# RWKV scan: inverse triangles multiplied in ahead of the recurrence, first inversion on VectorE, gate product inside the scan

## The chip, the cores and the metric

One core of a Trainium2 chip runs the whole program. The metric is the device time of one execution in microseconds (us); for one core that is the time from its first to its last instruction and what the launch adds to it. All arithmetic of the part in question is in fp32 (4 bytes); a few large products split each operand into a high and a low fp32r part and take three matmuls.

## The reference, cut to what matters

A two-block transformer on 512 tokens of width 1024 (and 256 context tokens). The change lies in one mixer of the second block, a bidirectional RWKV layer of 16 heads of size 64. What it computes per direction z, head h and token t (S is a 64x64 state):

```python
def _wkv_step(S, inp):
    r_t, w_t, k_t, v_t, a_t, b_t = inp
    sa = jnp.einsum('zbhvk,zbhk->zbhv', S, a_t)
    S = S * w_t[..., None, :] + sa[..., :, None] * b_t[..., None, :] + v_t[..., :, None] * k_t[..., None, :]
    return S, jnp.einsum('zbhvk,zbhk->zbhv', S, r_t)

def rwkv_out(y, h, xx, r, k_mod, v, mu, ln_g, ln_b, r_k, g1, g2, wo):
    y = layernorm(y, ln_g.reshape(RWKV_HEADS, RWKV_HEAD), ln_b.reshape(RWKV_HEADS, RWKV_HEAD), GN_EPS)
    bonus = jnp.einsum('bthk,zbthk->bth', _heads(r) * r_k, _heads(k_mod))
    y = y.astype(r.dtype) + bonus[..., None] * _heads(v)
    xg = h + xx * mu[5]
    gate = jax.nn.sigmoid(xg @ g1) @ g2
    return (y.reshape(bsz, n, d) * gate) @ wo
```

Here g1 is 1024 x 160 and g2 160 x 1024. The scan first runs over the 256 context tokens and goes on over the 512 tokens.

## The kernel before, in words

`rwkv_project` (L1913) forms r, k, v, q and the gate and stores them to DRAM, feature rows first, in the tensors `rw_r`, `rw_k` and so on. Its last piece is the gate: ACT takes the sigmoid of the 160 x 512 product (L2057), both factors are split into high and low parts, and for each of 8 blocks of 128 features PE runs 6 matmuls (L2074 to L2077), ACT copies the result (L2079) and SP stores it to `rw_g` (L2080).

`_RwkvScan` (L2107) then works in 8 head pairs p (128 features each). Tokens are cut in chunks of 64; 4 chunks make a unit, and a pair has three units u (0 is the context, 1 and 2 the tokens), so 12 chunk steps a pair and 96 in all. Inside a chunk the recurrence is solved in closed form, which needs the inverse of a unit lower triangle (64x64) for each chunk, direction and head.

- `pre` (L2288) makes the decayed operands AR and BK and the strict triangles of a pair; `load_tri` (L2397) brings the 32x32 diagonal blocks through DRAM into a layout of 96 partitions; `subst` (L2410) inverts them there in 31 dependent rounds of two instructions on GpSimd (POOL, L2420 and L2424, 62 instructions); `back` (L2427) returns them through DRAM to XT, and `merge` (L2442) builds the 64x64 inverses with 32x32 matmuls.
- `prep` (L2485) makes the products AAk and AAr of a unit, BKn by transposes, the values UV, and `intra` (L2548) multiplies AAk into UV: this is the right side of the chunk's system.
- `scan` (L2581) is the recurrence, a chain over engines: two matmuls of the state S with AR into `ry` (L2600, or L2605 in unit 0), a VectorE (DVE) add of the right side into `rz` (L2609), four matmuls with the inverse XT (L2616), an ACT copy into UV (L2620), four matmuls into the state's sums `sps` (L2625), and DVE's update of S with the decay (L2636, L2634 in a pair's first step). Beside the chain stand ACT's decayed copy (L2643), four matmuls that add the chunk's own part to `ry` (L2649) and the copy to yn (L2653).
- `out` (L2656) turns and normalises a finished pair, loads the pair's rows of `rw_g` (L2664) and multiplies (L2697).

The order of the work: `run` (L2128) emits the chain's pieces one by one at a high priority (offset 400) and, between them, the work of `beside` (L2156), that is the inversion, `pre`, `prep`, `merge` and `out` of neighbouring pairs; a scheduler then fixes one order for each engine, and every engine takes its instructions in that order. Before step 0 of a pair its `merge` has to be done. PSUM pools: ry 2, u 1, s 1, aa 2, tp 2 banks.

## Time and profile before

| what | value |
|---|---|
| median of 3 runs | 4190.04 us (4182.6 to 4209.11) |
| profiled execution | 4201.93 us |
| its span, first to last instruction | 4200.0 us |
| projections of the RWKV layer end, gate stage | about 2855 to 2880 us of the span |
| ahead of the first scan step | 2880 to 2978 us |
| scan steps of the 8 pairs | 2978 to 3587 us |
| PE busy share of the span | 90% |

Times in rows count from the span's start. PE is TensorE's matmuls, DVE VectorE, ACT ScalarE, POOL GpSimd; SPq is the queue that issues the DMAs. A busy PE includes the latency of its matmuls, and an fp32 matmul of this program shows as two records, so 8 records are 4 matmuls. "Clock" below is TensorE's granted clock: 1.00 is 2.4 GHz, 0.50 is 1.2 GHz.

### The profile page before, as it was taken

To read this page: it belongs to the slowest core of one execution; us is meant where nothing else is said; L and a number is where in the kernel's file an instruction comes from. 1 tells how busy PE (TensorE), PEld (TensorE's weight loads), DVE (VectorE), ACT (ScalarE), POOL (GpSimd) and SP (SyncE) were. 2 spreads that over 40 slices of the span, in tenths; PEclk is the share of its full clock that TensorE was granted. 3 is DMA by queue.
4 is the path that set the end of the run, shared out by engine and by line. 5 is a ranking of instruction groups with operands and counts; after the bars stand their busy time and mean duration, and the time that the engine had idled before them with its cause. 6 is when DMAs were issued, how large, how long until landed. Compare 5 with 4: busy or idle time off the path is not lost. (4 is left out here: it accounts for less than half of the span.)

```text
span 4200.0 us, 56465 instructions
## 1 busy us (share of the span) xinstructions
PE 3774.0 (90%) x22550; PEld 2588.1 (62%) x22550; DVE 1838.8 (44%) x3646; ACT 1322.6 (31%) x2612; POOL 683.8 (16%) x889
## 2 busy tenths in 40 slices
PE   7979999999999979998789997996788899688986
PEld 6747778756777869887333334774667777433332
DVE  3445345565534545334422225445657655511112
ACT  3334224344323433233111113424456555200001
POOL 1002000200201010001100002002555342200001
PEclk9969999999999989999899998997768769799998
DMA  3213553212452322122799996342211212499997
GB/s 110 81 38 117 182 192 105 81 32 76 144 179 82 101 70 68 52 102 79 294 406 391 398 404 236 93 152 66 54 40 43 60 48 79 185 394 415 415 413 306
DMA packets 324825, 711.86 MB, mean 169 GB/s; under 512 B 79616, under 2 KB 251904, under 8 KB 299728
## 3 DMA queue, kind: packets, MB, share of 16 engines
q1 hardware_dynamic: 308704, 658.43, 43.1%
q0 software_dynamic: 15856, 49.79, 3.4%
q8 instruction: 179, 2.93, 0.3%
q14 instruction: 86, 0.70, 0.1%
HBM read 666.64 MB, written 47.55 MB: 170 GB/s over the span
## 5 line engine op out<-in xcount | busy, mean ns | idle before, releaser
L266 PE MATMUL mmps<-xH,wH 128*128 128x512 f32 (+1 forms) x1384 | 552.0, 401 | 11.2 <-ACT xH L359 9.4
L268 PE MATMUL mmps<-xH,wL 128*128 128x512 f32 (+1 forms) x1384 | 543.9, 394 | 2.4 <-DVE wL L245 2.4
L267 PE MATMUL mmps<-xL,wH 128*128 128x512 f32 (+1 forms) x1384 | 544.8, 394 | 0.0
L1488 PE MATMUL bgps<-wg,bxT 128*64 128x512 f32 (+2 forms) x1040 | 471.5, 597 | 0.9 <-issue 0.9
L1489 PE MATMUL bgps<-wu,bxT 128*64 128x512 f32 (+1 forms) x896 | 398.2, 597 | 21.1 <-DMA wu<-in_moe_w_up_dram 20.8
L244 ACT ACTIVATE wH<-wraw 128x512 fp32r<-128x512 f32 (+3 forms) x473 | 265.0, 620 | 481.4 <-PE mmps L267 270.6
L245 DVE TENSOR_TENSOR wL<-wraw,wH 128x512 fp32r<-128x512 f32 (+3 forms) x473 | 328.6, 739 | 193.6 <-ACT wH L244 193.0
L266 PEld LDWEIGHTS mmps<-xH,wH 128*128 128x128 f32 (+1 forms) x1384 | 259.9, 188 | 92.4 <-ACT wH L244 12.4
L268 PEld LDWEIGHTS mmps<-xH,wL 128*128 128x128 f32 (+1 forms) x1384 | 259.9, 188 | 66.1 <-DVE wL L245 3.9
L1505 PE MATMUL byps<-wd,bhT 128*64 128x512 f32 (+2 forms) x1040 | 297.0, 658 | 1.1 <-ACT bhT L1496 1.1
L267 PEld LDWEIGHTS mmps<-xL,wH 128*128 128x128 f32 (+1 forms) x1384 | 260.2, 188 | 59.9 <-issue 1.4
L1488 PEld LDWEIGHTS bgps<-wg,bxT 128*64 128x64 f32 (+2 forms) x1040 | 139.0, 137 | 206.7 <-issue 200.3
L1490 ACT ACTIVATE bh<-bgps 64x512 f32<-64x512 f32 (+2 forms) x65 | 38.3, 590 | 641.2 <-PE bgps L1489 543.0
L1489 PEld LDWEIGHTS bgps<-wu,bxT 128*64 128x64 f32 (+1 forms) x896 | 111.9, 128 | 132.7 <-issue 91.6
L1491 DVE TENSOR_TENSOR bh<-bgps,bh 64x512 f32<-64x512 f32 (+1 forms) x56 | 38.6, 690 | 335.7 <-ACT bh L1490 335.7
L1505 PEld LDWEIGHTS byps<-wd,bhT 128*64 128x64 f32 (+2 forms) x1040 | 87.9, 147 | 157.8 <-issue 152.1
L2420 POOL TENSOR_TENSOR isub<-xT,rwX 96x31 f32<-96x31 f32 (+15 forms) x248 | 140.6, 567 | 262.0 <-DMA xT<-rwd 243.2
L1454 POOL DMA_INDIRECT xg<-hnat,ix x65 | 62.8, 967 | 640.1 <-PE bxps L1476 602.9
L2424 POOL TENSOR_TENSOR rwX<-rwX,isub 96x31 f32<-96x31 f32 (+15 forms) x248 | 155.5, 627 | 19.4
L2807 POOL TENSOR_TENSOR sqs<-sqs,sq 128x512 f32<-128x512 f32 (+1 forms) x60 | 82.3, 1372 | 392.8 <-ACT sq L2800 386.4
L266 PE MATMUL mmps<-mH,pH 128*128 128x512 f32 (+2 forms) x336 | 124.1, 372 | 12.0 <-ACT pH L244 9.1
L532 POOL TENSOR_TENSOR ffng<-ffng,rstd 128x512 f32<-128x512 f32 x44 | 57.8, 1316 | 452.2 <-ACT ffng L531 439.9
(746 smaller groups left out, 7529.6 us busy)
## 6 DMA issues: line engine op xcount, KB each, us to landing
wg<-in_moe_w_gate_dram SPq DMA_DIRECT2D x64, 2048.0 KB, 23.1
wu<-in_moe_w_up_dram SPq DMA_DIRECT2D x61, 2048.0 KB, 20.1
wd<-in_moe_w_down_dram SPq DMA_DIRECT2D x61, 2048.0 KB, 19.2
adaw<-in_ada_w_dram SPq DMA_DIRECT2D x48, 1024.0 KB, 5.0
wraw<-in_ffn_w_gate_dram SPq DMA_DIRECT2D x22, 1024.0 KB, 5.4
wraw<-in_ffn_w_up_dram SPq DMA_DIRECT2D x22, 1024.0 KB, 5.5
wraw<-in_ffn_w_down_dram SPq DMA_DIRECT2D x20, 1024.0 KB, 5.0
wraw<-in_ga_w_in_dram SPq DMA_DIRECT2D x16, 1024.0 KB, 5.5
```

The costliest lines, as they stand in the source:

```text
L244: self.nc.scalar.activation(H, src, AF.Copy)
L245: self.nc.vector.tensor_tensor(L, src, H.bitcast(F32), OP.subtract)
L266: nc.tensor.matmul(out, lh, rh, start=first, stop=False)
L267: nc.tensor.matmul(out, lh, rl, start=False, stop=False)
L268: nc.tensor.matmul(out, ll, rh, start=False, stop=last)
L1454: self.gathered = self.nc.gpsimd.indirect_dma_start(out=x[:m, :], out_offset=None, in_=hnat, in_offset=bass.IndirectOffsetOnAxis(ap=it, ax ...
L1488: nc.tensor.matmul(og, xT[:, k, :m], wg[:, k, :], start=k == 0, stop=k == KD - 1, skip_group_check=True)
L1489: nc.tensor.matmul(ou, xT[:, k, :m], wu[:, k, :], start=k == 0, stop=k == KD - 1, skip_group_check=True)
L1505: nc.tensor.matmul(o[j], hT[:, k, :m], wd[:, k, j * 512 : (j + 1) * 512], start=k == 0, stop=k == 3, skip_group_check=True)
L2420: G.tensor_tensor(o, Lt[:96, :j, j : j + 1].to_broadcast((96, j, n)), X[:96, j : j + 1, j:].to_broadcast((96, j, n)), OP.mult,)
L2424: G.tensor_tensor(X[:96, :j, j:], X[:96, :j, j:], o, OP.add)
L2807: K.nc.gpsimd.tensor_tensor(self.acc, self.acc, t, OP.add)
```

## The change

The inverse is no longer a link of the recurrence. For each unit, `prep` turns the state's operand by matmuls with the identity, multiplies the inverse into that operand (which is then copied back into AR) and into the right side UV (a new function `solve`), so that a chunk step goes from `ry` straight to `sps`: the add writes UV itself. Units 1 and 2 are solved inside `prep`, unit 0 behind `merge`. The first pair's inversion runs on DVE and not on POOL. The gate's second factor is no longer applied ahead of the scan: only the sigmoid (160 rows) is stored, and `out` multiplies it with 128 columns of g2 in two fp32 matmuls (128 and 32 rows deep). PSUM's u bank goes to tp.

```diff
@@ rwkv_project
-                nc.sync.dma_start(raw[: b - a], io["rw_g2"][a:b, :].rearrange("p (k f) -> p k f", f=P))
-                gate.append((b - a, sg, raw, wH, wL))
+                nc.sync.dma_start(dr["g"][a:b, :], sg[: b - a, :T])
...
-        for f in range(KD):
-            ps = self.pp.tile([P, 512], F32, tag="mm", name="mmps")
-            for i, (n, H, L, wH, wL) in enumerate(parts):
-                self.mm3(ps, wH[:n, f], wL[:n, f], H[:n, :T], L[:n, :T], i == 0, i == 1)
-            st = hp.tile([P, TA], F32, tag="st", name="st", bufs=3)
-            nc.scalar.activation(st[:, :T], ps, AF.Copy)
-            nc.sync.dma_start(dr["g"][f * P : (f + 1) * P, :], st[:, :T])
@@ _RwkvScan: pools, beside, setup, subst
-    NSCAN = 36
+    NSCAN = 24
-        self.pp = _Tagged(K.pool("rwps", space=PSUM, ctx=c), {"ry": 2, "u": 1, "s": 1, "aa": 2, "tp": 2})
+        self.pp = _Tagged(K.pool("rwps", space=PSUM, ctx=c), {"ry": 2, "s": 1, "aa": 2, "tp": 3})
...
+        if n == 0:
+            for _ in inv:
+                pass
+            self.back(0)
+            self.marks.add(("subst", 0))
...
-            mg = self.merge(n)
+            mg = (w for g in (self.merge(n), self.cur[n]["solve"]) for w in g)
...
-                with self.K.tc.high_priority(offset=400) if n == 7 else ExitStack():
+                with self.K.tc.high_priority(offset=400) if n in (0, 7) else ExitStack():
...
+        nc.sync.dma_start(self.glow, self.dr["g"][P:, :])
...
-        G, X, Lt = self.nc.gpsimd, self.X, self.Lt
+        G, X, Lt = self.nc.gpsimd if p else self.nc.vector, self.X, self.Lt
@@ prep, at the end of intra(u)
+            A.activation(I, ps, AF.Copy)
...
+                    PE.matmul(
+                        ps[64 * (1 - pr) : 64 * (1 - pr) + 64, (2 * z + m) * P : (2 * z + m + 1) * P],
+                        AR[:, 4 * z + j, (1 - pr) if u else 0, :], K.ident, start=True, stop=True, skip_group_check=True,
+                    )
+            V.tensor_copy(An, ps)
+            yield 0.6
+            L["solve"] = solve(u, An, I, UV)
+            if u:
+                yield from L["solve"]
+
+        def solve(u, An, I, UV):
+            XT, AR = L["XT"], L["AR"][u]
...
+                        PE.matmul(
+                            wps[j % 2][64 * h : 64 * h + 64, (2 * z + m) * 64 : (2 * z + m) * 64 + 64],
+                            An[r0 : r0 + 64, (2 * z + m) * P + 64 * h : (2 * z + m) * P + 64 * h + 64],
+                            XT[r0 : r0 + 64, u * 8 + z * 4 + h * 2 + m, :], start=True, stop=True, skip_group_check=True,
+                        )
...
+                        PE.matmul(
+                            ps[r0 : r0 + 64, o : o + 64], XT[r0 : r0 + 64, u * 8 + z * 4 + h * 2 + m, :],
+                            I[r0 : r0 + 64, o : o + 64], start=True, stop=True, skip_group_check=True,
+                        )
+            for q, w in enumerate(wps):
+                V.tensor_copy(AR[:, q::2, (1 - q) if u else 0, :], w[:, :256].rearrange("p (x i) -> p x i", i=64))
             A.activation(UV[64:, :, 0::2, :], p4[64:], AF.Copy)
             A.activation(UV[:64, :, 1::2, :], p4[:64], AF.Copy)
@@ scan
-                    V.tensor_tensor(rz[Uh], ry[Uh, :256].rearrange("p (z f) -> p z f", z=2), rhs, OP.add)
...
-                        PE.matmul(
-                            up[Uh, z * P + 64 * h : z * P + 64 * h + 64], XT[:, u * 8 + z * 4 + h * 2 + m, :],
-                            rz[:, z, 64 * h : 64 * h + 64], start=True, stop=True, skip_group_check=True,
-                        )
-                A.activation(rhs, up[Uh, :256].rearrange("p (z f) -> p z f", z=2), AF.Copy)
+                    V.tensor_tensor(uv, ry[Uh, :256].rearrange("p (z f) -> p z f", z=2), uv, OP.add)
@@ out
-        nc.sync.dma_start(gt, self.dr["g"][p * P : (p + 1) * P, :])
+        nc.sync.dma_start(gt, self.dr["g"][:P, :])
+        for t, a, b in ((g2, 0, P), (g2low, P, 160)):
+            nc.sync.dma_start(t, self.io["rw_g2"][a:b, p * P : (p + 1) * P])
...
-        V.tensor_tensor(yT, gt, yT, OP.mult)
+        ps = self.ps()
+        PE.matmul(ps, g2, gt, start=True, stop=False)
+        PE.matmul(ps, g2low, self.glow, start=False, stop=True)
+        V.tensor_tensor(yT, ps, yT, OP.mult)
```

Three places show how the order moves. In the changed kernel the line numbers are lower by 12 from `load_pre` to `products`, higher by 23 in `scan` and by up to 29 in `out`.

SP at the start of the scan, before (rw_g is the gate, ink, inq, inr and rwlora are what the first `pre` reads):

```order
L1986 DMA rw_r<-st 128x512 x5
L2080 DMA rw_g<-st 128x512 x8
L2241 DMA rwmask<-in_cst_dram 128x256
L2241 DMA rwflip<-in_cst_dram 128x128
L2241 DMA rwblk_19376<-in_cst_dram 128x128
L2242 DMA rwreset<-in_cst_dram 128x256
L2279 DMA ink<-rw_k 128x768
L2279 DMA inq<-rw_q 128x768
L2279 DMA inr<-rw_r 128x512
L2281 DMA rwloraw<-in_rw_w_dram 128x128
```

and now (rwX is the corner of a tile that holds the low 32 rows of the gate's first factor):

```order
L1987 DMA rw_r<-st 128x512 x5
L2059 DMA rw_g<-rwsg 128x512
L2059 DMA rw_g<-rwsg 32x512
L2228 DMA rwmask<-in_cst_dram 128x256
L2228 DMA rwflip<-in_cst_dram 128x128
L2228 DMA rwblk_19278<-in_cst_dram 128x128
L2229 DMA rwreset<-in_cst_dram 128x256
L2246 DMA rwX<-rw_g 32x512
L2267 DMA ink<-rw_k 128x768
L2267 DMA inq<-rw_q 128x768
L2267 DMA inr<-rw_r 128x512
L2269 DMA rwloraw<-in_rw_w_dram 128x128
```

The eight stores of the gate are gone; in their place stand two, and a load that reads one of them back stands ahead of the pair's loads.

DVE at the first inversion now (L2408 and L2412 are the inversion's two instructions, the others belong to `pre` of the second pair and `prep` of the first; before, POOL had the inversion and DVE's queue only the others):

```order
L2322 SCALAR_TENSOR_TENSOR cs<-rwreset,sg 128x256 x2
L2408 TENSOR_TENSOR isub<-xT,rwX 96x31
L2323 TENSOR_TENSOR sg<-cs,sg 128x512
L2412 TENSOR_TENSOR rwX<-rwX,isub 96x31
L2563 COPY AAk<-rwtpps 128x512
L2408 TENSOR_TENSOR isub<-xT,rwX 96x60
L2336 TENSOR_TENSOR km<-km,ink 128x256
L2412 TENSOR_TENSOR rwX<-rwX,isub 96x30x2
L2336 TENSOR_TENSOR km<-km,ink 128x256
L2408 TENSOR_TENSOR isub<-xT,rwX 96x87
```

The inversion begins behind the work already queued and alternates with 33 other instructions up to its 34th; the rest of it stands alone.

DVE between the last state update of unit 0 (L2636, L2659 now) and the add of unit 1's first step (L2609, L2643 now), in a middle pair. Before:

```order
L2636 SCALAR_TENSOR_TENSOR S<-rwsps,P,SP 128x128 x2
L2335 TENSOR_TENSOR sg<-cs,sg 128x512
L2347 SCALAR_TENSOR_TENSOR bb<-th,inq 128x256
L2348 TENSOR_TENSOR km<-km,ink 128x256
L2349 SCALAR_TENSOR_TENSOR BK<-bb,E_23697 128x4x128
L2353 SCALAR_TENSOR_TENSOR ARc<-inq,sg 128x256 x2
L2359 TENSOR_TENSOR BK<-km,E_23697 128x4x2x64
L2609 TENSOR_TENSOR rwrz_19395<-rwryps,UV 64x256
```

and now (L2594 is the solved operand's copy, L2703 and L2705 the statistics of `out`):

```order
L2659 SCALAR_TENSOR_TENSOR S<-rwsps,P,SP 128x128 x2
L2347 TENSOR_TENSOR BK<-km,E_23946 128x4x2x64
L2594 COPY ARl<-rwtpps 128x4x64 x2
L2369 TENSOR_TENSOR xT<-rwaaps,rwmask 128x2x128 x2
...
L2322 SCALAR_TENSOR_TENSOR cs<-rwreset,sg 128x256 x2
L2336 TENSOR_TENSOR km<-km,ink 128x256
L2703 BN_STATS gbs<-AAk 128x6 x8
L2705 BN_AGGR gmv<-gbs 128x2 x8
L2323 TENSOR_TENSOR sg<-cs,sg 128x512
...
L2347 TENSOR_TENSOR BK<-km,E_24109 128x4x2x64
L2708 RECIPROCAL grs<-grs 128x8
L2643 TENSOR_TENSOR UV<-rwryps,UV 64x2x128
```

More than twice the work now stands between the two instructions of the chain.

## Rows read from the trace of the kernel before

**Rows 1.** Stretches: us, busy us (instructions) of PE, PEld, DVE, ACT, POOL, clock, DMA.
```profile
2855.00:2888.00 33.00, 21.33 (x49) 11.00 (x48) 2.95 (x8) 8.36 (x14) 1.69 (x4) 0.63 0.37 129
...
2921.00:2978.00 57.00, 32.47 (x443) 27.76 (x443) 41.46 (x66) 20.00 (x41) 41.01 (x68) 0.62 0.22 50
2978.00:3587.00 609.00, 559.31 (x6375) 440.75 (x6376) 372.26 (x951) 340.23 (x762) 264.48 (x443) 0.80 0.20 52
```

**Rows 2.** Timeline of the gate stage: start, duration, engine, line, instruction.
```profile
2856.01 1.06 ACT L2057 ACTIVATE rwsg<-thps 128x512 f32<-128x512 f32 x2
...
2879.34 0.60 ACT L2079 ACTIVATE st<-mmps 128x512 f32<-128x512 f32 x1 [2.56 <-PE mmps L268]
...
2888.38 1.22 PE L2309 MATMUL rwtpps<-rw_tw,rwloraw 64*128 64x256 f32 x4 [9.12 <-DMA rwloraw<-in_rw_w_dram]
```

**Rows 3.** Timeline of POOL, first and last instruction of the first inversion.
```profile
2921.25 0.25 POOL L2420 TENSOR_TENSOR isub<-xT,rwX 96x31 f32<-96x31 f32 x1 [40.60 <-DMA xT<-rwd]
...
2964.53 0.24 POOL L2424 TENSOR_TENSOR rwX<-rwX,isub 96x31 f32<-96x31 f32 x1
```

**Rows 4.** Timeline of DVE, ahead of the first inversion: prices of two sizes.
```profile
2893.61 0.40 DVE L2348 TENSOR_TENSOR km<-km,ink 128x256 f32<-128x256 f32 x1
2893.93 0.68 DVE L2335 TENSOR_TENSOR sg<-cs,sg 128x512 f32<-128x512 f32 x1
```

**Rows 5.** Timeline of one chain step of the last pair, clock 1.00.
```profile
3561.87 0.61 DVE L2636 SCALAR_TENSOR_TENSOR S<-rwsps,P,SP 128x128 f32<-128x128 f32 x2
...
3563.72 0.57 PE L2616 MATMUL rwups<-rwrz,rwXT 128*64 128x64 f32 x7
...
3564.39 0.38 ACT L2620 ACTIVATE UV<-rwups 64x256 f32<-64x256 f32 x1 [0.98 <-PE rwups L2616]
...
3565.46 0.61 DVE L2636 SCALAR_TENSOR_TENSOR S<-rwsps,P,SP 128x128 f32<-128x128 f32 x2 [0.42 <-PE rwsps L2625]
```

**Rows 6.** Timeline of DVE, state updates of the fourth and fifth pair, and one add.
```profile
3213.31 0.61 DVE L2634 TENSOR_SCALAR S<-rwsps,P 128x128 f32<-128x128 f32 x2 [2.82 <-PE rwsps L2625]
...
3226.29 0.59 DVE L2636 SCALAR_TENSOR_TENSOR S<-rwsps,P,SP 128x128 f32<-128x128 f32 x2
...
3288.03 0.61 DVE L2634 TENSOR_SCALAR S<-rwsps,P 128x128 f32<-128x128 f32 x2 [4.59 <-PE rwsps L2625]
...
3308.53 0.61 DVE L2636 SCALAR_TENSOR_TENSOR S<-rwsps,P,SP 128x128 f32<-128x128 f32 x2 [1.14 <-ACT UV L2620]
...
3315.06 0.43 DVE L2609 TENSOR_TENSOR rwrz<-rwryps,UV 64x256 f32<-64x256 f32 x1
...
3370.01 0.61 DVE L2634 TENSOR_SCALAR S<-rwsps,P 128x128 f32<-128x128 f32 x2 [4.58 <-PE rwsps L2625]
```

**Rows 7.** Timeline of PE, the nearest shapes to those that go and come.
```profile
3344.72 0.68 PE L2616 MATMUL rwups<-rwrz,rwXT 128*64 128x64 f32 x8
3345.33 0.57 PE L2376 MATMUL rwaaps<-ARl,BK 64*64 64x64 f32 x22
...
3091.53 1.34 PE L2566 MATMUL rwtpps<-kms,rwblk 128*128 128x512 f32 x2
```

**Rows 8.** Stretches of the fourth and fifth pair, columns as in rows 1.
```profile
3213.00:3227.00 14.00, 13.85 (x153) 10.31 (x152) 9.52 (x25) 9.09 (x22) 11.23 (x22) 1.00 0.11 32
3288.00:3309.00 21.00, 21.00 (x141) 14.90 (x141) 9.07 (x24) 8.05 (x19) 18.80 (x29) 0.54 0.06 19
...
3350.00:3355.00 5.00, 2.89 (x53) 2.29 (x54) 4.73 (x14) 4.34 (x10) 0.00 (x0) 1.00 0.52 139
3355.00:3360.00 5.00, 4.48 (x90) 4.03 (x88) 2.48 (x5) 0.35 (x1) 0.00 (x0) 0.50 0.50 111
```

**Rows 9.** Groups of PE in the scan (2978 to 3587): busy, mean | idle before them.
```profile
L2616 PE MATMUL rwups<-rwrz,rwXT 128*64 128x64 f32 x768 | 78.2, 257 | 18.2 <-DVE rwrz L2609 17.9 <-ACT rwXT L2479 0.3
...
L2625 PE MATMUL rwsps<-UV,BKn 128*64 128x64 f32 x704 | 46.8, 262 | 6.8 <-ACT UV L2620 6.7
...
L2376 PE MATMUL rwaaps<-ARl,BK 64*64 64x64 f32 x384 | 13.8, 255 | 3.7 <-DVE xT L2381 3.7
```

More of the change, by code (lines that the diff above doesn't have):

```diff
@@ L1882, in rwkv @@
             dp = self.pool("rwdram", space=DRAM, ctx=c)
[L1883 removed]
+            dr = {n: dp.tile([D, TA if n in "kvq" else T], F32, name=f"rw_{n}") for n in ("r", "k", "v", "q", "y")}
+            dr["g"] = dp.tile([160, T], F32, name="rw_g")
             dr["x"] = dp.tile([P, KD * T], F32, name="rw_x")
@@ L2139, in run @@
             for i in range(self.NSCAN):
-                need = {("prep", p, i // 12), ("merge", p), ("out", p - 1) if i >= 12 else ("merge", p)}
+                need = {("prep", p, i // 8), ("merge", p), ("out", p - 1) if i >= 8 else ("merge", p)}
                 while not need <= self.marks:
@@ L2144, in run @@
                     next(sc)
-                if i % 12 == 11:
-                    self.marks.add(("scan", p, i // 12))
+                if i % 8 == 7:
+                    self.marks.add(("scan", p, i // 8))
                 goal += 100 / self.NSCAN
@@ L2255, in setup @@
         self.X = one("X", 32, 32)
+        low = self.X[96:].rearrange("p s t -> p (s t)")
+        self.glow, self.g2low = low[:, :T], low[:, T:].rearrange("p (n f) -> p n f", f=P)
+        nc.sync.dma_start(self.glow, self.dr["g"][P:, :])
         self.lora = [one(f"lora{n}", P) for n in "wa"]
-        self.rz = [one(f"rz{i}", 2, P) for i in range(2)]
-        for t in self.rz:
-            nc.gpsimd.memset(t, 0.0)
         self.sps = self.ps("s")
@@ L2560, in intra @@
                 yield 0.85
+            flat = AAk.rearrange("p x m q i -> p (x m q i)")
+            An, I = flat[:, :512], flat[:, 512:]
+            A.activation(I, ps, AF.Copy)
+            ps = self.ps()
+            AR = L["AR"][u]
+            for z in range(2):
+                for j in range(4):
+                    m, pr = j // 2, j % 2
+                    PE.matmul(
[9 more added lines that the diff above has]
+            XT, AR = L["XT"], L["AR"][u]
+            wps = [self.ps() for _ in range(2)]
+            for z in range(2):
+                for j in range(4):
+                    m, r0 = j // 2, 64 * (1 - j % 2)
+                    for h in range(2):
+                        PE.matmul(
[3 more added lines that the diff above has]
+                        )
+            yield 0.9
+            ps = self.ps()
+            for z in range(2):
+                for h in range(2):
+                    for j in range(4):
+                        m, r0 = j // 2, 64 * (1 - j % 2)
+                        o = (2 * z + m) * P + 64 * h
+                        PE.matmul(
[4 more added lines that the diff above has]
+                V.tensor_copy(AR[:, q::2, (1 - q) if u else 0, :], w[:, :256].rearrange("p (x i) -> p x i", i=64))
             p4 = ps.rearrange("p (z m f) -> p z m f", z=2, m=2)
```

26 lines of the change are left out of this document (5 added, 21 removed).

## The prediction

> **What bounds the kernel now.** I read the stretches first, then the timelines of the three places that the diff touches, then PE's groups. In the scan (2978 to 3587) PE is busy 559 of 609 us at a mean clock of 0.80; DVE has 372, ACT 340 and POOL 264 [rows 1]. PE leaves 50 us idle, and much of it stands in the chain: 18.2 us ahead of the matmuls with the inverse (the wait for DVE's add) and 6.8 us ahead of the state matmuls (the wait for ACT's copy) [rows 9]. So the scan is mostly PE's, in its order, with the chain's latencies between the pieces. The reader should also see that the clock matters as much as the work: three steps take 13.0 us in the fourth pair (3213.31 to 3226.29) at clock 1.00, and 20.5 us in the fifth (3288.03 to 3308.53) at 0.54, with PE busy nearly throughout in both [rows 6, 8]. That is 2.5 us a step. One such fall follows a stretch in which PE is busy for 2.89 of 5 us: 1.00 there, 0.50 in the next stretch, although PE is busy again [rows 8].
>
> Ahead of the scan two stages are chains. The gate's product runs from the end of the sigmoid, 2857.07, to ACT's last copy, 2879.94, at a mean clock of 0.63; the scan's first matmul follows at 2888.38, having waited for a load [rows 1, 2]. POOL's first inversion runs from 2921.25 to 2964.77, 43.5 us [rows 3], and nothing of the first pair's scan can start without it; in that stretch DVE is busy 41.5 of 57 us with the first pairs' own preparation [rows 1].
>
> **The change part by part.**
>
> *Gate.* Eight blocks of product, copy and store go from the path; two stores remain, of the sigmoid's output. The path now leaves at 2857.07 and not at 2879.94, 22.9 us earlier. Against that, SP has the read-back of 32 rows ahead of the pair's loads, and it waits for a store. Between the last copy and the first matmul lay 8.44 us before, which held an issue and a load [rows 2]; I price the read-back's wait at 2 us and take **-21** (ends -23 with no wait, -14.5 if it costs a whole such interval again).
>
> *First inversion.* By size it gains: 62 instructions over 10,912 elements a partition in all. DVE's 0.40 us for 256 elements and 0.68 for 512 [rows 4] give 1.09 ns an element and 0.12 us an instruction, so 11.9 + 7.4 = 19.3 us in place of 43.5. But DVE is not free. In its order the inversion begins behind queued work and alternates with 33 other instructions. At 0.40 to 0.68 us these are 13 to 22 us, say 15, as many are small; and I put 11 us on what is queued ahead of it, from DVE's 41.5 busy us in that stretch [rows 1]: 19.3 + 15 + 11 = 45 and some waiting among the others for PE and ACT, so about 46.5. **+3** (ends -24 if the queue has drained, +14 if it waits through all of DVE's 41.5 us).
> The Trainium skill ("GPSIMD Engine Reference", section 4.1, Engine selection) says that two-input elementwise work runs about twice as slowly on GpSimd as on VectorE; the prices above agree roughly, 43.5 against 19.3. By that rule alone the stage would lose an estimated 22 us and the sum below would be 25 lower; the row on DVE's load is why I don't take it.
>
> *First solve.* Unit 0 of the first pair is solved behind its merge, on the path: two groups of matmuls, a copy on DVE of 0.40 us and a second one behind it [rows 4]. **+2** (0 to +4).
>
> *PE in the scan, what goes.* The matmuls with the inverse: 78.2 us busy, and the 6.8 us of PE's wait for ACT's copy [rows 9]. PE's 18.2 us of waiting for the add do not go: the state matmuls now stand behind that same add. **-85** (ends: -50, the bare work of 384 matmuls at the 0.13 that two records take where they run close, 0.68 us for 8 records [rows 7]; and -101, if all 96 steps shorten by the whole link. That link, in a step at clock 1.00, runs from PE's start at 3563.72 to the end of ACT's copy at 3564.77, or 1.05 us of a step of 3.59 [rows 5]).
>
> *PE, what comes.* 16 quadrant matmuls for the operand and 16 for the right side in each of 24 units: 768, or 1536 records. The nearest group of 64x64 quadrants is busy 13.8 us for 384 records, 0.036 each [rows 9]: +55. 8 transposing matmuls in each unit, 192 in all, of 128 columns, no such shape being in the rows: by columns each is four of those records, 0.14 us, and four of the records of 0.68 / 8 us are 0.34 [rows 7]; I take 0.2, +38 (ends +27 and +65). 16 gate matmuls of 512 columns: 1.34 us for a pair of records with its latency [rows 7], I take 1.25, +20. **+113** (ends +102, and +217 with every record at 0.085 and every gate matmul at 1.34: 131 + 65 + 21).
>
> *PE's idle time.* Of the 50 us, 43 are left after the copy's wait is gone. Between two links of the chain PE had 559 / 288 = 1.9 us of work; it gets (559 - 78 + 113) / 192 = 3.1 us, against a link of 3.59 / 3 = 1.2 us [rows 1, 5]. So most waits inside steps should close; those at pair boundaries stay. **-30** (0 to -43).
>
> *DVE in the scan.* 24 copies of 512 elements and 48 of 256: 35 us more, on 372. It matters in one place. Between the last update of unit 0 and the add of unit 1's first step DVE had 6.5 us (3308.53 to 3315.06) [rows 6], and the order now has more than twice the work there, at about 10 us undisturbed. PE has more work for that stretch too, so I count 2 us a pair for 7 pairs: **+14** (0 to +45). ACT gives up 96 copies of 0.38 us [rows 5] for 24 longer ones and is no bound. The new loads of g2 and the sigmoid are hidden by a DMA share of 0.20 [rows 1].
>
> Sum: -21 + 3 + 2 - 85 + 113 - 30 + 14 = -4. Counted by the chain instead, half the 96 steps get shorter by the link (-50), and the bare PE work grows by +113 less 384 x 0.13 / 0.80 = 62, or 51: with the rest of the list -21 + 3 + 2 - 50 + 51 + 14 = -1; with that growth half hidden in gaps it is -26. I take -10, between the three. The profiled execution took 4201.93 us, the median is 4190.04: the difference goes on the median, **4180**. What a measurement of this kernel tells from no change is about 1%, 42 us, so this is no change.
>
> **The rivals.**
>
> *A, the chain bounds every step (faster).* The whole link goes 96 times, -101; of the 51 us of bare new work about 30 lie at boundaries and cost, the rest lies in gaps; ahead of the scan -16: 4190 - 87 = **4103**. For it: the 25 us of PE's waits that stand in the chain, and a PE that with fewer gaps may keep clock 1.00 longer. Against it: 559 of 609 busy [rows 1].
>
> *B, DVE starves PE at unit 1's first step and the clock falls (slower).* The place is the one above: PE waits behind DVE's block in every pair, its busy share drops as it did before 3355, and the steps that follow run at half clock, 2.5 us dearer each [rows 6, 8]. With 5 of the 7 later steps at half clock in 7 pairs, +87, in place of the +14: 4166 + 87 = **4253**. It decides from 4 of 7 steps on (4166 + 70 = 4236). For it: the block has more than doubled, and the scan has spent part of its time at half clock already. Against it: PE has more to do beside the wait.
> The Trainium skill ("TensorE: Matmul & The Clock Gate", Part 1, What's actually happening) says the throttled state is the default and activity releases it. The 0.50 behind a stretch of little work agrees; the 0.54 with PE busy all of 21 us [rows 8] does not sit easily with it, so I don't rest more than a chance on this.
>
> *C, PE is the bound everywhere.* No idle time closes, since the work that comes lies at the boundaries, where PE is already the limit: 4180 + 30 = **4210**, and more if small groups do not overlap: one quadrant record shows a mean of 255 ns [rows 9]. If each of three new groups in 24 units laid one such latency bare, +18: 4228.
> The Trainium skill ("TensorEngine Tiling (Array Packing)", Key Properties) speaks against the change here: a change of tiling mode drains TensorE, and the new groups change it often. The trace shows little of it: the quadrants that start at 3345.33 follow matmuls of another mode that run from 3344.72 to 3345.40 [rows 7].
>
> *D, DVE is free for the inversion.* -24 in place of +3: **4153**, still within 1%.
>
> **How the numbers follow.** Forecast 0.38, A 0.25, B 0.20, C 0.12, D 0.05. A's cases lie below 4148 nearly all (0.24), and the forecast's lower edge adds 0.08: faster 0.32. Slower than 4232 are most of B (0.17) and a part of C and of the forecast's upper edge (0.05): 0.22. The rest, 0.46, is within 1%. The likeliest case by itself spans 4150 to 4220. The range leaves a tenth at each side: 4105 (near A) to 4250 (near B).
>
> **What would show it.** First matmul of the scan near 2867; the inversion on DVE 45 us long from the landing of its triangles to its end; per pair about 80 us as before; PE's idle time in the scan below 25 us; busy time of the quadrant groups near 55 us. Pairs of 70 us with a clock of 0.9 would mean A; a PE gap of over 5 us at unit 1's first step with 0.50 behind it, B; an inversion of under 25 us, D. I would be wrong most plainly if the mean clock in the scan moved far from 0.80, for my prices are taken at that clock.

## The result and the profile after

| | median us | runs | range | ratio to before (95% interval) |
|---|---|---|---|---|
| before | 4194.91 | 7 | 4182.6 to 4209.11 | |
| changed | 4231.52 | 7 | 4218.08 to 4234.44 | 1.0085 (1.0062 to 1.0108) |

The change costs 0.85%, some 36 us. The forecast was 10 us faster with a range of 4105 to 4250: the time lies within the range and within 1%, but it moved the other way, and clearly so. The profiled execution of the changed kernel took 4218.08 us, the fastest of its seven, and that of before lies 7 us above its median, so the two traces differ by 16.3 us of span where the medians differ by 36.6. The table below can place only those 16 us; where the other executions lose the rest no trace shows.

**Where the time goes.** For a table of the pairs I take from DVE's timeline the starts of the state updates S and of the adds: "unit 0" is from a pair's first to its fourth S, "S to add" from there to unit 1's first add, "units 1, 2" from that add to the pair's last add, "boundary" from there to the next pair's first S.

| us | before | changed |
|---|---|---|
| first S of the scan | 2980.9 | 2962.8 |
| pair 1, pair 2 (first S to first S) | 68.7, 84.2 | 86.6, 97.7 |
| pairs 3 to 6, mean of a pair | 79.6 | 78.9 |
| of it: unit 0 | 18.7 | 10.0 |
| S to add | 5.8 | 15.2 |
| units 1, 2 | 35.1 | 32.2 |
| boundary | 20.0 | 21.5 |
| pairs 7 and 8, to the last add | 131.6 | 137.7 |
| last add | 3583.8 | 3600.6 |

So the stage ahead of the scan gains 18 us, the first two pairs lose 31, four middle pairs gain 3 in all, the last two lose 6. Unit 0 is almost twice as fast, and the stretch behind it takes all of that back. Not all of unit 0's gain is the shorter chain: at clock 1.00 its three steps took 13.0 us before (fourth pair) and take 9.4 and 9.1 now (third and sixth), some 4 us of the 8.7. The rest is the clock, which stood at 0.52 to 0.53 in three of these four units 0 before, and is at 1.00, 0.91, 0.64 and 1.00 now.

Ahead of the scan, the timelines of ACT and PE in the changed kernel's gate stage (start, duration, engine, line, instruction, idle time before and what ended it), to be read against [rows 2]:

```profile
2857.95 1.06 ACT L2058 ACTIVATE rwsg<-thps 128x512 f32<-128x512 f32 x2
...
2867.25 1.23 PE L2297 MATMUL rwtpps<-rw_tw,rwloraw 64*128 64x256 f32 x4 [9.88 <-DMA rwloraw<-in_rw_w_dram]
```

The scan's first matmul starts 21.1 us earlier than the 2888.38 of [rows 2], as the sum had it. Next the first inversion, now on DVE, and the second on POOL, in place of [rows 3]:

```profile
2908.15 0.18 DVE L2408 TENSOR_TENSOR isub<-xT,rwX 96x31 f32<-96x31 f32 x1
...
2942.21 0.19 DVE L2412 TENSOR_TENSOR rwX<-rwX,isub 96x31 f32<-96x31 f32 x1
...
2947.07 0.24 POOL L2408 TENSOR_TENSOR isub<-xT,rwX 96x31 f32<-96x31 f32 x1
...
2985.74 0.24 POOL L2412 TENSOR_TENSOR rwX<-rwX,isub 96x31 f32<-96x31 f32 x1
```

The first takes 34.3 us, from 2908.15 to 2942.40; the second runs to 2986.0. It is the second that the scan waits for. The timelines of SP's queue, ACT, DVE and PE in the middle of the first pair (a row of SPq is the issue of a DMA):

```profile
2986.02 0.32 SPq L2419 DMA_DIRECT2D rwd<-rwX  x1
2989.01 0.30 SPq L2425 DMA_DIRECT2D rwXT<-rwd  x1
2989.41 0.46 SPq L2273 DMA_DIRECT2D inv<-rw_v  x1
...
2993.57 0.84 ACT L2481 ACTIVATE vrev<-inv 128x768 f32<-128x768 f32 x1 [22.16 <-DMA inv<-rw_v]
2994.32 0.61 ACT L2326 ACTIVATE sg<-sg 128x512 f32<-128x512 f32 x1
...
2994.96 0.76 DVE L2341 SCALAR_TENSOR_TENSOR ARc<-inq,sg 128x256 f32<-128x256 f32 x2 [19.76 <-ACT sg L2326]
...
2995.44 1.13 PE L2364 MATMUL rwaaps<-ARc,BK 64*64 64x64 f32 x30 [23.66 <-DVE ARc L2341]
```

Read from the top: SP issues the store of the second inverse when POOL is done, and only behind it the load of v for the second pair. ACT has that load's consumer at the head of its queue, the exponential `sg` stands behind it, DVE's ARc waits for `sg`, PE for ARc, and unit 1 of the first pair stands behind all of them. POOL's inversion has become a link of the scan. Before, SP issued the same load 30 us ahead of that store:

```profile
2988.76 0.34 SPq L2285 DMA_DIRECT2D inv<-rw_v  x1
3018.37 0.31 SPq L2431 DMA_DIRECT2D rwd<-rwX  x1
```

In the changed kernel's second pair the store of the next inverse holds the store of y, and with it DVE (same columns):

```profile
3096.24 0.32 SPq L2419 DMA_DIRECT2D rwd<-rwX  x1
...
3099.74 0.53 SPq L2728 DMA_DIRECT2D rw_y<-AAk  x1
...
3102.21 0.42 DVE L2513 TENSOR_TENSOR AAk<-rwaaps,rwmask 128x256 f32<-128x256 f32 x1 [12.46 <-DMA rw_y<-AAk]
...
3103.27 0.79 PE L2634 MATMUL rwryps<-S,ARl 128*128 128x128 f32 x2 [11.82 <-DVE S L2659]
```

The scan as a whole (stretch from first S to last add, columns as in [rows 1]):

```profile
2962.80:3600.60 637.80, 518.75 (x7471) 407.36 (x7472) 411.86 (x1015) 316.70 (x685) 248.45 (x419) 0.86 0.19 50
```

Between the same two points before, from 2980.9 to 3583.8, PE was busy 553.2 of 602.9 us. PE has more records now and is busy 34 us less, at a clock of 0.86 in place of 0.80; and its idle time has gone from 50 to 119 us. The groups of PE in the changed kernel from 2978 to 3600, its scan but for the first 15 us, show both halves (busy, mean ns | idle before):

```profile
L2504 PE MATMUL rwaaps<-ARl,BK 64*128 64x128 f32 x448 | 50.8, 303 | 1.0 <-DVE AAr L2515 1.0
L2648 PE MATMUL rwsps<-UV,BKn 128*64 128x64 f32 x672 | 47.7, 252 | 55.3 <-DVE UV L2643 55.1
...
L2589 PE MATMUL rwtpps<-AAk,rwXT 64*64 64x64 f32 x736 | 34.4, 253 | 1.6 <-ACT rwXT L2467 1.4
...
L2577 PE MATMUL rwtpps<-rwXT,AAk 64*64 64x64 f32 x736 | 24.3, 252 | 0.5
...
L2559 PE MATMUL rwtpps<-ident,ARl 128*64 128x128 f32 x240 | 21.4, 300 | 0.0
```

As many records of the first row's product were busy 76.8 us before:

```profile
L2516 PE MATMUL rwaaps<-ARl,BK 64*128 64x128 f32 x448 | 76.8, 398 | 0.5 <-DVE xT L2381 0.5
```

At either level of the clock a record of this product takes the same in both traces, 0.42 us at 0.50 and 0.27 at 1.00 in the median; what moved is how many stand at 0.50, 278 of 448 before and 35 of 464 in the whole scan now. The state matmuls wait 55 us for the add, where [rows 9] had 18.2 and 6.8 us for the link that is gone. One of these waits, in the fifth pair, on PE and DVE:

```profile
3320.96 0.61 PE L2634 MATMUL rwryps<-S,ARl 128*128 128x128 f32 x4
3321.50 1.11 PE L2510 MATMUL rwaaps<-ARc,BK 64*128 64x64 f32 x16
3330.60 0.69 PE L2648 MATMUL rwsps<-UV,BKn 128*64 128x64 f32 x8 [7.99 <-DVE UV L2643]
...
3319.77 0.73 DVE L2335 SCALAR_TENSOR_TENSOR bb<-th,inq 128x256 f32<-128x256 f32 x1 [1.69 <-ACT th L2304]
...
3327.92 1.10 DVE L2337 SCALAR_TENSOR_TENSOR BK<-bb,E 128x512 f32<-128x512 f32 x1
3328.94 1.03 DVE L2347 TENSOR_TENSOR BK<-km,E 128x512 f32<-128x512 f32 x1
3329.90 0.19 DVE L2708 RECIPROCAL grs<-grs 128x8 f32<-128x8 f32 x1
3330.12 0.43 DVE L2643 TENSOR_TENSOR UV<-rwryps,UV 64x256 f32<-64x256 f32 x1
```

The product that the add needs is done at 3321.6. The add starts at 3330.1, behind DVE's block, in which a 128x512 instruction takes 1.0 to 1.1 us where [rows 4] shows 0.68. Behind this wait the clock is at its lower level. The 10 us from the add on, before and then changed, in the fifth pair (columns as in [rows 1]):

```profile
3315.10:3325.10 10.00, 8.53 (x63) 7.15 (x63) 7.30 (x31) 6.44 (x13) 8.52 (x18) 0.62 0.00 1
```

```profile
3330.10:3340.10 10.00, 8.81 (x49) 5.05 (x51) 8.25 (x19) 1.47 (x3) 7.58 (x17) 0.50 0.04 11
```

In pairs 2 to 6 these 10 us stood at 0.60, 0.50, 0.94, 0.62 and 0.61 before, and are at 0.50, 0.75, 0.50, 0.50 and 0.50 now. The mean rose all the same: in unit 0, and at the boundary, where it was 0.72, 0.89, 0.65, 0.65 and 0.64 and is now 0.81 and four times 1.00.

### The profile page after: what moved, and what is told of

It is laid out like the page before. It is cut to its first block, busy times and chain, and to the rows that moved or that the text cites. A ratio compares the mean times of both kernels' runs of the same rounds, so it can differ in the third digit from the quotient of the medians.

```text
span 4216.3 us, 58725 instructions
## 1 busy us (share of the span) xinstructions
PE 3717.4 (88%) x23686; PEld 2551.6 (61%) x23686; DVE 1881.5 (45%) x3770; ACT 1293.7 (31%) x2528; POOL 639.7 (15%) x823
## 5 line engine op out<-in xcount | busy, mean ns | idle before, releaser
L2408 POOL TENSOR_TENSOR isub<-xT,rwX 96x31 f32<-96x31 f32 (+15 forms) x217 | 123.7, 570 | 258.7 <-DMA xT<-rwd 242.1
L2412 POOL TENSOR_TENSOR rwX<-rwX,isub 96x31 f32<-96x31 f32 (+15 forms) x217 | 131.3, 605 | 17.0
L1495 PEld LDWEIGHTS bhps<-ident,bh 64*128 64x128 f32 (+2 forms) x260 | 35.9, 209 | 144.8 <-DVE bh L1491 144.8
## 6 DMA issues: line engine op xcount, KB each, us to landing
wu<-in_moe_w_up_dram SPq DMA_DIRECT2D x61, 2048.0 KB, 19.3
```

Source lines behind the costliest of these rows:

```text
L2408: G.tensor_tensor(o, Lt[:96, :j, j : j + 1].to_broadcast((96, j, n)), X[:96, j : j + 1, j:].to_broadcast((96, j, n)), OP.mult,)
L2412: G.tensor_tensor(X[:96, :j, j:], X[:96, :j, j:], o, OP.add)
```

## The experiments

Each is compared with runs of the kernel before on the same chip (medians there 4196.73 to 4200.21 us). The intervals reach some 7 to 13 us to either side, and 24 and 33 for e11 and e8, which have two executions each; e14 has four, the others six to twelve. "Queue" in the table means that the store of the inverse and its loads are issued from POOL's queue.

| | edit | median us | ratio (95% interval) |
|---|---|---|---|
| e1 | gate part only | 4189.89 | 0.9981 (0.9962 to 1.0000) |
| e2 | first inversion on DVE only | 4214.51 | 1.0023 (0.9999 to 1.0047) |
| e3 | solve only | 4226.36 | 1.0078 (1.0049 to 1.0106) |
| e4 | changed + queue | 4204.25 | 1.0020 (1.0003 to 1.0037) |
| e5 | e4, out split | 4222.23 | 1.0063 (1.0036 to 1.0090) |
| e6 | e4, first inversion on POOL | 4202.28 | 1.0019 (0.9991 to 1.0047) |
| e7 | before + queue | 4201.23 | 1.0018 (0.9988 to 1.0049) |
| e8 | e4 without POOL's rounds | 4137.35 | 0.9866 (0.9788 to 0.9943) |
| e9 | e4, priority offset 250 | 4199.37 | 1.0010 (0.9984 to 1.0036) |
| e10 | e4, priority offset 700 | 4222.19 | 1.0051 (1.0023 to 1.0080) |
| e11 | before without POOL's rounds | 4126.70 | 0.9831 (0.9774 to 0.9889) |
| e12 | e4, solve's copies on ACT | 4194.31 | 1.0001 (0.9976 to 1.0027) |
| e13 | e12 with offset 250 | 4188.31 | 0.9987 (0.9966 to 1.0009) |
| e14 | changed, v load from ACT's queue | 4218.23 | 1.0065 (1.0042 to 1.0087) |
| e15 | gate part + queue | 4182.77 | 0.9962 (0.9937 to 0.9986) |

**The three parts alone (e1 to e3).** Each takes the hunks of the diff that belong to one part: e1 those of `rwkv_project`, `out` and the load into glow, e2 those that put the first inversion on DVE and its store ahead of the rest (two of them below), e3 all that is left.

```diff
-        G, X, Lt = self.nc.gpsimd, self.X, self.Lt
+        G, X, Lt = self.nc.gpsimd if p else self.nc.vector, self.X, self.Lt
...
+        if n == 0:
+            for _ in inv:
+                pass
+            self.back(0)
+            self.marks.add(("subst", 0))
```

> Only the gate part of the change on the kernel before. Theory 1 (the loss of the whole change is made by SP's queue and DVE's queue, not by PE's work): the stage ahead of the scan gets 21 us shorter as in the changed kernel (first matmul of the scan 2867.25 in place of 2888.38), the 16 gate matmuls cost a few us beside other work, so 4195 - 21 + 5, about 4179, between 4170 and 4188. Theory 2 (PE is the bound and each added matmul costs its time): the 16 matmuls give 20 us back, 4194 within 5.

Measured 4189.89, 8 us faster by the ratio: outside theory 1 and at the edge of theory 2's number, which does not show theory 2's reason. The first S of the scan stands at 2958.4 in its trace, 22.5 us earlier than before, but its scan is 608.3 us long in place of 602.9. It also gives POOL's inversion its own time with the gate gone: 2897.87 to 2941.59.

> Only the first inversion on DVE, with the gate and the recurrence of the kernel before. Theory 1: the inversion itself is 9 us shorter (34.3 us measured in the changed kernel against 43.5), but the second inversion now starts on POOL at once, its store waits in SP's queue ahead of the second pair's v load (the order has the store before the load here too), and ACT, DVE and PE wait for that load: a stall of about 20 us inside the first pair. Net no gain or a loss: 4195 to 4210. Theory 2: nothing else moves, and the gain of 9 to 22 us stays: 4173 to 4186.

Measured +0.23% by the ratio, 10 us, with an interval that just reaches no change, and 4214.51 by the median, a little more than theory 1 had; the gain of theory 2 is not there. In its first pair an S stands 15.6 us behind its add (3002.4 to 3018), where the kernel before has no gap over 5 us in that pair; DVE waits there for the v load, issued at 3013.41 behind the second inverse's store at 3012.99. The first S is not earlier but 7 us later (2988.2). This trace is of the slowest of the ten executions.

> Only the inverse multiplied into the operand and the right side, with the gate and the inversion on POOL of the kernel before. Theory 1: unit 0 of each pair gets some 8 us shorter, the step at which unit 1 begins some 8 us longer since DVE's block there has grown from 7 instructions to 34; 4195 to 4212, with no stall above 10 us in the first two pairs. Theory 2 (PE's added work is the bound): +28 us by the groups of PE or more, 4223 or above.

Measured +0.78%, 33 us: theory 2's number. But not its reason. In the trace the middle pairs are 77.9 us, 1.7 shorter than before; pairs 1 and 2 are 7 and 11.5 us longer, with a stall of 17.7 us in the second, at 3098, where DVE waits 16.59 us for the store of y and that store is issued behind the inverse's at 3111. Theory 1's "no stall above 10 us" is wrong: the stall of the second pair comes with the solve alone. The three parts add up to -8 + 10 + 33 = +35, the whole change, though each of them is known to 10 us only, and the waits on SP's queue are in e2 and in e3.

**The queue (e4, e7, e14, e6).**

```diff
     def back(self, p):
...
-        nc.sync.dma_start(d2, self.X[:96])
+        nc.gpsimd.dma_start(d2, self.X[:96])
...
-                nc.sync.dma_start(
+                nc.gpsimd.dma_start(
                     XT[rows, :, 32 * b : 32 * b + 32],
```

> The changed kernel with the store of the inverse and its four loads issued from POOL's queue and not from SP's. Nothing of the computation differs. Theory 1: the v load, the loads of g2 and the store of y no longer stand behind a store that waits for POOL's inversion; the stall of 23.7 us in the first pair and that of 11.8 us in the second go, 4231 - 35, about 4196, between 4185 and 4206. Theory 2 (PE's work is the bound): within 10 us of 4231.

Measured 4204.25, within what theory 1 had; by the ratios 1.0085 and 1.0020 the move is worth 27 us. The first pair falls from 86.6 to 77.5 us, the second from 97.7 to 91.1, together 16 us; the rest of the 27 has no place in the traces, which differ by 13 us of span, the changed kernel's being its fastest execution. The stall of the second pair did not go: an 11.9 us gap is left there, now behind DVE's wait for the loads of the inverse itself.

In e7 the same two lines are changed in the kernel before.

> The kernel before with the inverse's store and loads issued from POOL's queue. Theory 1 (e4 gained because in the changed kernel other transfers stand behind that store): before, the second v load was issued 30 us ahead of the store, and little stands behind it; 4197 within 6. Rival (POOL's queue is better for these transfers anyway): 10 us or more faster, 4187 or below, and then e4's gain is no proof of the stall.

Measured no change: before, nothing that matters stood behind that store. So e4's gain is the removal of a wait that the change had made.

```diff
-        self.nc.sync.dma_start(v, self.dr["v"][p * P : (p + 1) * P, :])
+        self.nc.scalar.dma_start(v, self.dr["v"][p * P : (p + 1) * P, :])
```

> The changed kernel with nothing moved but the load of v, which ACT's queue issues in place of SP's. Theory queue: the stall of 23.7 us in the first pair goes, that of 11.8 us in the second (the store of y behind the same inverse) stays: 4231 - 22, about 4209, between 4200 and 4217. Rival (the stall only moves, as ACT itself waits for something else of that time): within 8 us of 4231.

Measured 13 us by the medians, just outside what was expected. Of the first pair's stretch of 28.9 us from S to add, 19.4 remain, and the timelines of SP, DVE and PE in e14 say why:

```profile
2982.41 0.32 SPq L2419 DMA_DIRECT2D rwd<-rwX  x1
2985.40 2.01 SPq L2425 DMA_DIRECT2D rwXT<-rwd  x4
...
2989.09 0.98 DVE L2437 STREAM_TRANSPOSE XoP<-rwXT 128x768 f32<-128x768 f32 x1 [10.33 <-DMA rwXT<-rwd]
2989.99 0.72 DVE L2594 COPY ARl<-rwtpps 128x256 f32<-128x256 f32 x2
...
2990.43 1.22 PE L2634 MATMUL rwryps<-S,ARl 128*128 128x128 f32 x4 [9.99 <-DVE ARl L2594]
```

With the load out of the way, DVE's queue has the next pair's merge ahead of the copy that unit 1 needs, and the merge waits for the same inverse. The second pair's stall, which I expected to stay, went too (85.2 us in place of 97.7). The trace shows why: in the changed kernel the load that POOL's third inversion waits for stands behind a v load on SP's queue (issued at 3051.35, right behind the 3050.83 of the v load); here it goes out at 3036.13, the third inverse's store at 3082.02 in place of 3096.24, and DVE waits 3.05 us for the store of y in place of 12.46.

e6 is e4 without the hunks of e2.

> The kernel of e4 with the first inversion on POOL again. In the gate-only kernel POOL's inversion ran from 2897.9 to 2941.3, in the changed kernel DVE's from 2908.2 to 2942.4: by theory 1 the choice of engine is worth about a microsecond and the time stays within 6 us of 4204. Rival (the inversion on DVE delays the first pairs' other work on DVE, which e2 could mean by its +10): 4194 or lower.

As theory 1: the engine of the first inversion is worth nothing that can be measured, once nothing stands behind the second.

**The stretch behind unit 0 (e5, e9, e10, e12, e13).** In e4 the middle pairs take 78.0 us: 9.4 in unit 0, 15.6 from S to add, 30.6, and 22.5 at the boundary. PE is busy 521.7 of 620.9 us in its scan, so 99 us are idle, and 58.2 of them are waits of the state matmuls for the add.

e5 leaves only the first piece of `out` ahead of unit 1:

```diff
             if p > 0:
-                yield from self.out(p - 1)
+                late = self.out(p - 1)
+                yield next(late)
                 self.marks.add(("out", p - 1))
...
                 self.marks.add(("prep", p, 2))
+            if p > 0:
+                yield from late
```

> The kernel of e4 in which only the first piece of out (the transposes that read yn) stays ahead of unit 1, and its statistics, scaling and gate product come behind the preparation of unit 2. DVE's block between the last update of unit 0 and unit 1's first add falls from 32 instructions to 19 in the order. Theory 1 (DVE's queue holds the chain there): that stretch falls from 15.5 us to about 11 in five pairs, PE's wait for the add from 39.5 us over four pairs to below 25, and the time from 4204 to about 4189, between 4180 and 4197. Rival: PE's work or ACT holds the chain there, and the time stays within 5 us of 4204.

A miss: 18 us slower. The state matmuls' waits for the add fall from 58.2 to 12.0 us in the whole scan (another 12 us wait for an add stands ahead of the matmuls of L2675), but the stretch keeps its length (15.8), and the boundary grows to 25.6. DVE and PE in the fifth pair of e5:

```profile
3323.97 0.86 DVE L2338 SCALAR_TENSOR_TENSOR bb<-th,inq 128x256 f32<-128x256 f32 x1
3324.76 2.02 DVE L2325 TENSOR_TENSOR_SCAN cs<-rwreset,sg 128x256 f32<-128x256 f32 x2
...
3329.97 0.68 DVE L2566 COPY AAk<-rwtpps 128x512 f32<-128x512 f32 x1
...
3333.10 0.43 DVE L2646 TENSOR_TENSOR UV<-rwryps,UV 64x256 f32<-64x256 f32 x1
...
3330.80 0.89 PE L2580 MATMUL rwtpps<-rwXT,AAk 64*64 64x64 f32 x32 [4.05 <-DVE AAk L2566]
```

Fewer instructions stand ahead of the add, but they are the long ones, of the next pair's `pre`; and PE now waits, in its own order, for DVE's copy An of the following solve, 19.8 us in the scan. Counting instructions of the order was the wrong measure.

e9 and e10 change the priority of the chain's pieces in `run` (700 in e10):

```diff
-                with self.K.tc.high_priority(offset=400):
+                with self.K.tc.high_priority(offset=250):
                     next(sc)
```

> The kernel of e4 with the priority offset of the chain's pieces at 250 in place of 400. In the order DVE's instructions ahead of the four adds of unit 0 and the first of unit 1 become 9, 12, 2 and 11 in place of 2, 1, 2 and 32 in the middle pairs. Theory (the chain of unit 0, now short, runs ahead of the solve of unit 1, and then waits for it and for DVE's block): unit 0 gets longer by some 6 us, the stretch to unit 1's first add shorter by more, about 9; pairs 2 to 5 at 74 us in place of 77.8, the time about 4185, between 4175 and 4197. Rival (the sum of the work on DVE and PE between the chain's pieces sets the pair, and where it lies is one): the stretches change, the period does not, 4204 within 6.

Measured 4199.37. The stretches moved as expected (unit 0 16.6, S to add 8.6 us), the period only from 78.0 to 75.8. The time is within the rival's 6 us of 4204. Its reason is not shown: the period did change, and the scan in e9's trace is 608.0 us long where e4's is 620.9. That trace is of the fastest of e9's ten executions, so how much of the difference is the edit stays open.

> The kernel of e4 with the offset at 700. DVE has 14 instructions ahead of unit 1's first add in place of 32, and 26 ahead of the first add of unit 2 in place of about 1. Theory of e9: the wait is moved to unit 2 and its size stays: within 8 us of 4204. Rival (unit 1's stretch is special, for out and the solve of unit 1 meet there): 4 us a pair gained in six pairs, 4180 or below.

Measured 4222.19, 18 us slower, which neither theory had. A wait went to unit 2 (up to 21.1 us ahead of an add there), and the one ahead of unit 1 only fell from 15.6 to 13.3 us; where it lies does matter, but nowhere tried is it free.

e12 moves the three copies of each solve to ACT:

```diff
-            V.tensor_copy(An, ps)
+            A.activation(An, ps, AF.Copy)
...
-                V.tensor_copy(AR[:, q::2, (1 - q) if u else 0, :], w[:, :256].rearrange("p (x i) -> p x i", i=64))
+                A.activation(AR[:, q::2, (1 - q) if u else 0, :], w[:, :256].rearrange("p (x i) -> p x i", i=64), AF.Copy)
```

> The kernel of e4 with the three copies of the solve per unit (An and the two halves of AR) on ACT in place of DVE. DVE loses about 35 us of its 415 in the scan, ACT gains as much on 316. Theory DVE (DVE's queue holds the chain between unit 0 and unit 1): the block falls from 32 to 27 instructions, and 20 us are gained, 4204 - 20, about 4184, between 4172 and 4194. Theory PE (the pair is set by PE's work and the links of the solve, whichever engine copies): within 6 us of 4204.

Measured 4194.3, 10 us better, between the two. S to add falls from 15.6 to 14.2 us, the period from 78.0 to 77.1.

> As e12, with the priority offset of e9 (250). Theory DVE: e9 and e12 add up, 4199 - 20, about 4180. Theory PE: as e9, 4199 within 6.

Measured 4188.3, again between the two; together with e9's offset the copies bring another 11 us, and the middle pairs are at 73.6 us, 6 below the kernel before. What is lost lies at the ends: pairs 1 and 2 take 176.3 us there, 152.9 before.

**POOL beside the rest (e8, e11).** Both leave out the inversion's rounds of pairs 1 to 7 (counted from 0).

```diff
-        for j in range(31, 0, -1):
+        for j in range(31, 0 if p == 0 else 31, -1):
```

> The kernel of e4 without the inversion's rounds for pairs 1 to 7 (POOL only clears the tile and sets the diagonal), so the inverses of these pairs are left out. Theory 1 with a second cause (DVE's instructions are stretched while POOL works beside them): DVE's 128x256 instructions in the block fall from 0.7 us to 0.42 and the 128x512 ones from 1.1 to 0.7, the stretch to unit 1's first add falls from 15.5 to about 11 us in six pairs, 4204 - 27, about 4177 or below. Rival (POOL does not matter to DVE): durations as they are, within 8 us of 4204.

> The kernel before without the inversion's rounds on POOL for pairs 1 to 7 (the inverses of these pairs are left out), the counterpart of e8, which was 67 us below e4. Theory (the change made the chain depend on DVE, which is slower beside POOL, and so the changed kernel loses more to POOL): a smaller gain here, 4198 - 30, about 4168, between 4155 and 4180. Rival (POOL costs both kernels the same): 4198 - 67, about 4131, within 12.

Both kernels gain some 70 us (e8 4204 to 4137, e11 4200 to 4127), so no run shows that the change has made the kernel more sensitive to POOL, and the rival of e11 holds. Two stretches that hold the scan, e8 first and then e11, columns as in [rows 1]:

```profile
2966.00:3530.00 564.00, 513.18 (x7608) 406.36 (x7603) 372.31 (x1046) 319.53 (x695) 29.52 (x46) 0.92 0.21 59
```

```profile
2960.00:3530.00 570.00, 523.17 (x6670) 411.60 (x6670) 358.16 (x1001) 342.78 (x771) 19.63 (x36) 0.90 0.24 64
```

From first S to last add DVE completes 1015 instructions in 364 us of busy time in e8 and 1014 in 415 in e4; the clock is 0.92 in the row and 0.86 in e4's scan. The 15 us from S to add did not shrink, though, against the expectation: in a middle pair 37 instructions of DVE stand there in place of 31. These kernels also have their inverses earlier, so the 70 us are not the price of POOL's company alone.

**A version that beats both (e15).**

> The gate-only kernel of e1 with the inverse's store and loads on POOL's queue. In e1 the two loads of g2 per pair stand behind the inverse's store in SP's queue, and 13 of the 21 us were lost again. Theory queue: those come free, 4199 - 18, about 4181, between 4172 and 4188. Rival (the 13 us are the price of the 16 gate matmuls and of out's longer chain): 4191 within 4, as e1.

Measured 4182.77, ratio 0.9962 (0.9937 to 0.9986): 16 us faster than before, 50 faster than the change. The gate part is worth keeping; against e1 alone the intervals overlap, so the share of the queue in it is not shown.

e15 also gives the price of the solve itself, for e6 differs from it by the solve alone: both have the gate part, the first inversion on POOL and the moved queue. Their ratios, 0.9962 (0.9937 to 0.9986) and 1.0019 (0.9991 to 1.0047), lie some 24 us apart. So taking the inverse out of the chain loses time even with no store of an inverse on SP's queue. In the two traces it gains 14 us in pairs 3 to 6 (81.1 us a pair in e15, 77.6 in e6) and loses 17 in the first two pairs and 11 in the last two; PE's idle time in the scan is 51 us in e15 and 103 in e6.

## Why the prediction was wrong, step by step

Two steps failed. The waits on SP's queue stood at nothing in the sum, and cost 27 us; PE's idle time was to fall by 30 us, and rose by 69. By the runs the change is made of the gate part with the queue moved (-16, e15), the engine of the first inversion (nothing, e4 against e6), the solve (+24, e6 against e15) and the queue (+27, changed against e4), each known to some 10 to 15 us. The sum had -1 for the gate part (-21, and +20 for its matmuls), +3, -6 for the solve (2 - 85 + 93 - 30 + 14) and 0 for the queue. That the time still lies within the range is in part luck: in the traces of e15 and e6 the solve takes 37 us off PE's busy time, where some 15 were to come, and this hides much of the idle time, which rises by 52 and was to fall.

- *Gate, -21.* Right for its stage: 21.1 us at the scan's first matmul, though the 2 us taken off were not the read-back. From the end of the sigmoid, 2859.01, to the matmul are 8.24 us, as short as the 8.44 of before, and the sigmoid itself ends 1.9 us later than before. The gain doesn't come through whole: e1 gains 8.
- *First inversion, +3.* Right as far as it went. DVE starts 10.3 us behind where POOL starts in e1 (I had 11 us of queue), runs 34.3 us (I had 19.3 + 15) and ends 0.8 us later. In e2, with the gate of before, the inverse's store is issued 3.1 us later than before (2967.86, 2964.80). (The end of +14 does not come out of its own terms: 19.3 + 41.5 would be +17.) The failed part is what I did not price: the second inversion now follows at once on POOL, its store comes ahead of the v load on SP, and PE stands idle for 24 us of the first pair. With nothing behind the store (e4) the engine makes no difference (e6).
- *"The new loads of g2 and the sigmoid are hidden by a DMA share of 0.20."* This step failed, with its neighbours on SP. The share was 0.19 in the changed kernel's scan, and it says nothing on an order: what counted is which wait stood ahead. SP has the store of the second inverse ahead of the v load and a later one ahead of the store of y, and the prediction weighed only the rows of SP at the start of the scan. e4 measures the sum of these waits at 27 us, e7 shows that the queue move itself gives nothing that can be measured.
- *First solve, +2.* e3's first S is 4.3 us later than before, which is the upper end.
- *PE, -85 and +113.* The new groups measure, over the whole scan, 34.4 + 24.3 + 30.4 (both forms of the transposing matmuls) + 23.4 (gate) = 112: right. The sum is not: PE's busy time fell by 34. The groups that the change leaves alone fell from 582 to 517 us in sum: 37% of their records stood at the clock's lower level before, and 13% do now. The prediction named the clock as what would break its prices, and it did. (One price was misread: 0.68 us for 8 records is 0.17 for two and not 0.13, so 384 matmuls are 65 us and not 50, and the count by the chain would have come to -21 in place of -1, further from what was measured.)
- *PE's idle time, -30.* Wrong in sign, and this is the other step that failed. I let the shorter chain close the waits inside steps. It did shorten unit 0, whose three steps fell from 18.7 to 10.0 us, about half of it by the clock; but unit 0 now arrives before unit 1 is ready, and the stretch behind it went from 5.8 to 15.2. Idle time went from 50 to 119 us, and is still 99 in e4.
- *DVE's block, +14.* The place was right (unit 1's first step). The size was 9.4 us a pair and not 2, most of it paid by unit 0's gain. Rival B named this place, and its sign is in the trace: a gap of 7.7 to 8.3 us on PE at this step in each of pairs 2 to 6, and a clock of 0.50 in the 10 us behind it in four of them. Its price is not, since most of these stretches stood at 0.50 to 0.62 before as well and the mean clock of the scan rose; so B had the place and the wait, and not the cost. Rival A's shorter steps were real, and were spent at that wait. Rival C's bound, PE, is not it: PE is idle for 119 of 638 us.

What stays open: which engine owns the middle pairs in e4. Taking work off DVE (e12) gains half of what it should if DVE were alone, fewer instructions in the block (e5) lose, and moving the chain against the rest (e9, e10) trades one stretch for another. Open too is why the solve's 24 us are lost in the first two pairs and the last two, where e13 and e6 have them. A version in which unit 1's solve is done a pair ahead was not run.

## What to carry to other kernels

In this kernel a load and a store became dear because a store ahead of them on their queue waited for a slow engine: read the issuing queue's order as closely as an engine's, above all where a part of the change starts a slow producer earlier. A link taken out of a recurrence is a gain only up to the next thing that the chain needs; ask when that is ready, and compare it with the time at which the shorter chain arrives. Where TensorE's busy time is priced from rows at a middling clock, the price was good here for the new work but not for the total, since the clock moved the unchanged groups (-65 us) by more than the balance of the work that came and went (+112 and -76).

## What the runs showed of the hardware

- DVE's two-input instructions on 128x256 (bb, L2335) take 0.41 to 0.43 us in the changed kernel's scan where POOL does nothing beside them, and up to 0.90, with a median of 0.71, beside POOL's rounds; in e8, where POOL is almost idle, 0.41 to 0.43. Copies of 128x512 out of PSUM (AAk, L2563) take 0.67 to 0.69 us with POOL beside them and without. One of the changed kernel without POOL, to be read against the 0.73 at 3319.77 above, and one of e8:

```profile
3351.89 0.41 DVE L2335 SCALAR_TENSOR_TENSOR bb<-th,inq 128x256 f32<-128x256 f32 x1
```

```profile
3194.76 0.42 DVE L2335 SCALAR_TENSOR_TENSOR bb<-th,inq 128x256 f32<-128x256 f32 x1 [3.01 <-ACT th L2304]
```

The Trainium skill ("SBUF — State Buffer", section "SBUF: two separate sides") describes a port pair that DVE's two-input instructions and GpSimd take in turns, each for a whole instruction; the stretched durations agree with that.
- PE's granted clock and its busy share do not go together in these rows: 0.54 with PE busy 21 of 21 us before [rows 8], and 1.00 with 6.5 of 9 us busy in the changed kernel (unit 0 of the sixth pair):

```profile
3383.00:3392.00 9.00, 6.50 (x130) 5.06 (x134) 8.48 (x21) 6.06 (x15) 8.10 (x11) 1.00 0.15 44
```

What makes the difference no run here isolates.
